# Two buffers for the gate and value rows of a gated MLP's up projection, and their two-column copies on ScalarE

## The chip, the cores and the metric

The kernel runs on one core of a Trainium2 chip. The metric is the device time of one execution in microseconds (us). In the views below PE is TensorE's matmul queue, PEld its weight loads, DVE VectorE, ACT ScalarE, POOL GpSimd and SP the engine that issues the DMAs. L256 is line 256 of the kernel.

## The reference, cut to what matters

One decoder layer: attention and RWKV heads, an output projection, and then a gated MLP with a causal convolution of width 3 over the sequence. The change lies in the MLP alone:

```python
def conv_gated_ffn(h, w_up, conv_w, conv_b, w_down):
    S = h.shape[1]
    u = h @ w_up
    u_pad = jnp.pad(u, ((0, 0), (CONV_WIDTH - 1, 0), (0, 0)))
    u = conv_b + sum(conv_w[j] * u_pad[:, j:j + S] for j in range(CONV_WIDTH))
    gate, val = jnp.split(u, 2, axis=-1)
    return (jax.nn.gelu(gate, approximate=True) * val) @ w_down
```

Sequence 2048, model width 1024, hidden width 4096 for the gate and 4096 for the value, all float32. A float32 product is made of three matmuls on a high and a low part of each operand.

## The kernel before, in words

Phases a and b (projections, attention, RWKV, output projection) fill the first 1200 us. Phase d is the MLP: the up projection until about 2527 us, then the down projection. A framework builds the program: it orders the instructions of each engine by its own scheduler, gives tiles their buffers from pools, and sets the semaphores. Each engine then runs its list in order.

The up projection goes in two halves of the sequence (1024 columns each), and in each half over 32 blocks of 128 hidden features. So there are 64 blocks n. A block has a gate row tile `ug` and a value row tile `uv`, each 128 x 1026: two columns of the half before (the halo of the convolution), then 1024 columns of this half. The 2 x 2 block products are replaced by seven products per block (j = 0 to 6, a Strassen-like scheme), made in the order SEQU = 0, 1, 2, 3, 5, 4, 6. A product (L250) is 12 matmuls of 128x512 into one PSUM bank, so a block is 84 matmuls. Two blocks are interleaved, the second half a block behind the first.

- `wprep(n, j)` prepares the weights of a product: GpSimd makes sums and differences of the loaded weights `wr` (L218, L219, L224, L227), `split` makes a high part on ScalarE (L40, `wh`) and a low part on VectorE (L41, `wl`). It is called 5 products ahead (LEAD). The parts of j = 0, 1, 4, 5 lie in the pool `dwl`, the others in `dwr`.
- `post(n, j)` empties the bank. j = 0, 2, 3: ScalarE copies it to `sum` (L280). j = 1 and 4: VectorE adds `sum` and the bank into the halves of `ug` (L276). j = 5: the same into the second half of `uv`. j = 6 adds to the bank that j = 5 left, and ScalarE copies it to the first half of `uv` (L290). So the product j = 6 of a block can't start before the L276 that reads j = 5 from the same bank.
- `utile(n, b)` takes a buffer for `ug` (b = 0) or `uv` (b = 1) and copies the two halo columns into it (L256). `conv(n, b)` saves the last two columns of the row for the next half (L264, first half of the sequence alone, n < 32), then forms the convolution: ScalarE one tap (L266), VectorE two taps (L267, L268). The gate goes through GELU on ScalarE (L286), and VectorE multiplies gate and value (L293). For each pair of blocks GpSimd and VectorE also form sums for the down projection (L305 to L308).

`ug` and `uv` have one buffer each, in the pool `du`. So `utile` of a block waits for `conv` of the block before to have read the row.

In the first four blocks GpSimd also forms sums of the second half's input (`hsum`, L77 to L83: a load `hs`, four operations, a store). Around the change of the halves (n = 31) the input parts `hh` and `hl` are made anew, by larger splits.

Of the kernel before, what the change touches and what calls it, by code (L numbers as in the profile page):

```python
# [101 lines left out]
def phase_d(ctx, tc, x1, h2t, w_up, cw, halo, w_down, g_post, mhalf, out, hq, act, td):  # L102
# [5 lines left out]
    nc = tc.nc  # L108
    SB = 1024
    NU = FF // P  # L110
    with ExitStack() as es:


        pool = lambda name, bufs=1, side="left": es.enter_context(tc.tile_pool(name=name, bufs=bufs, side=side))
        hrp, wrp, wsp = pool("dr", 2), pool("drw", 2), pool("dsw", 3)
        wps = {"left": pool("dwl", 5)}
        bps = {i: pool(f"d{i}", side="left" if i < 8 else "right") for i in range(14)}
        wps["right"] = pool("dwr", 4, "right")
        up_, ep = pool("du", side="right"), pool("de", side="right")
        pss = [es.enter_context(tc.tile_pool(name=f"dp{i}", bufs=1, space=PSUM)) for i in range(8)]  # L120
        w0c, w1c, w2c, bc = (cw[:, i * 64:(i + 1) * 64] for i in range(4))

# [53 lines left out]
        with ExitStack() as us:  # L176
# [76 lines left out]
            def utile(n, b):  # L253
                col = b * NU + n % NU
                u = up_.tile([P, SB + 2], F32, name="ug" if b == 0 else "uv")
                nc.vector.tensor_copy(out=u[:, 0:2], in_=halo[:, col, :])  # L256
                us_[n, b] = u
                return u

            def conv(n, b):  # L260
                col = b * NU + n % NU
                u = us_.pop((n, b))
                if n < NU:
                    nc.vector.tensor_copy(out=halo[:, col, :], in_=u[:, SB:])  # L264
                y = tp.tile([P, SB], F32, name="yg" if b == 0 else "yv", bufs=3 - 2 * b)
                nc.scalar.activation(out=y, in_=u[:, 2:], func=AF.Identity, scale=w2c[:, col:col + 1], bias=bc[:, col:col + 1])  # L266
                nc.vector.scalar_tensor_tensor(out=y, in0=u[:, 1:SB + 1], scalar=w1c[:, col:col + 1], in1=y, op0=ALU.mult, op1=ALU.add)  # L267
                nc.vector.scalar_tensor_tensor(out=y, in0=u[:, 0:SB], scalar=w0c[:, col:col + 1], in1=y, op0=ALU.mult, op1=ALU.add)  # L268
                return y

            def post(n, j):
# [9 lines left out]
                elif j == 1:  # L281
                    add(utile(n, 0)[:, 2:514], sums.pop((n, 0)), b)
                elif j == 4:
                    add(us_[n, 0][:, 514:], sums.pop((n, 2)), b)
                    ys[n] = conv(n, 0)
                    nc.scalar.activation(out=ys[n], in_=ys[n], func=AF.Gelu_apprx_tanh)  # L286
                elif j == 5:
                    add(utile(n, 1)[:, 514:], sums.pop((n, 3)), a)
                else:
                    nc.scalar.copy(out=us_[n, 1][:, 2:514], in_=a)  # L290
                    yv = conv(n, 1)
                    y = ys.pop(n)
                    nc.vector.tensor_tensor(out=y, in0=y, in1=yv, op=ALU.mult)  # L293
                    k, m = ff // 4, ff // 2 % 2
                    dst = act[half][k][:, m].rearrange("j p t -> p j t")
                    if ff % 2 == 0:
                        nc.sync.dma_start(out=dst[:, 4], in_=y[:, :512])
                        even[0] = y
                        return
                    nc.sync.dma_start(out=dst[:, 5:7], in_=y.rearrange("p (j t) -> p j t", j=2))  # L300

                    e = even.pop(0)
                    s = hrp.tile([P, 4, 512], F32, tag="hr", name="sa")
                    V, Q = nc.vector.tensor_tensor, nc.gpsimd.tensor_tensor
                    Q(out=s[:, 2], in0=e[:, :512], in1=e[:, 512:], op=ALU.subtract)  # L305
                    V(out=s[:, 0], in0=e[:, 512:], in1=y[:, 512:], op=ALU.add)  # L306
                    V(out=s[:, 1], in0=s[:, 0], in1=e[:, :512], op=ALU.subtract)  # L307
                    Q(out=s[:, 3], in0=y[:, :512], in1=s[:, 1], op=ALU.subtract)  # L308
                    nc.sync.dma_start(out=dst[:, 0:4], in_=s)
# [855 lines left out]
def hybrid_layer(ctx, tc, a, c, out):  # L1165
# [25 lines left out]
    phase_b(ctx, tc, s, x, a["w_out"][0], a["norm_mix_post"], a["norm_ffn_pre"], a["sinks"], c["tri"], ident, mhalf, gc, line, x1, h2t, hq[0],  # L1191
            cw, a["conv_w"][0], a["conv_b"][0])
    phase_d(ctx, tc, x1, h2t, a["w_ffn_up"][0], cw, halo, a["w_ffn_down"][0], a["norm_ffn_post"],
            mhalf, out[0], hq, act, td)

# [38 lines left out]
```

## Time and profile before

| | |
|---|---|
| median of 3 runs | 3162.61 us (3157.29 to 3166.73) |
| the profiled execution | 3158.45 us |
| its span on the core | 3156.6 us |
| mean granted clock of TensorE | 0.978 of full speed |
| busy: PE, DVE, ACT, POOL | 3043.6, 2302.4, 1448.5, 1098.2 us |
| share of the span | 96%, 73%, 46%, 35% |

A matmul record is longer than the distance between two matmuls, since they overlap: a busy PE is not a PE at its peak. So the text below counts distances between starts. In a timeline each row has the start, the duration, engine, line and operation, and in brackets the idle time of that engine just before it, with what ended it.

### The profile page before, as it was taken

The page shows a single profiled execution, that of the slowest core. Times are in us where ns is not written, and L with a number is a line of the kernel's source. Part 1 is how long each engine was busy: PE and PEld are TensorE (multiplying, and loading weights), DVE is VectorE, ACT ScalarE, POOL GpSimd, SP SyncE. Part 2 cuts the span into 40 slices and gives each one's busy share as a digit, 9 for nine tenths or more (in the row PEclk, how much of TensorE's full clock was granted, in tenths as well). Part 3 has the DMA queues.
Part 4 walks back from the last instruction along what each step waited for, and adds up shares of the span by engine and source line. Part 5 has one row for each costly group of instructions (what it writes and reads, how often), then busy time and mean ns, then how long its engine had stood idle before and what let it go on. Part 6 is the DMA issues. An engine that isn't in the chain of part 4 may idle for free.

```text
span 3156.6 us, 46475 instructions
## 1 busy us (share of the span) xinstructions
PE 3043.6 (96%) x17897; PEld 2458.3 (78%) x17897; DVE 2302.4 (73%) x3170; ACT 1448.5 (46%) x2438; POOL 1098.2 (35%) x903
## 2 busy tenths in 40 slices
PE   8999999979999998899999999999999999999997
PEld 6788888767777776778787877888887788888786
DVE  6778787766767666999998998888888843334555
ACT  6465756344444445444444445444444432333332
POOL 2212112123323523554444443444444420003642
PEclk9999999969999999999999999999999999999999
DMA  5736363653445635433333343333333474446764
GB/s 162 195 123 187 114 170 104 186 169 108 130 123 161 201 92 196 153 118 101 101 101 101 115 150 123 100 100 100 100 103 101 160 267 151 149 140 227 279 214 167
DMA packets 523762, 461.14 MB, mean 146 GB/s; under 512 B 117306, under 2 KB 405396, under 8 KB 522516
## 3 DMA queue, kind: packets, MB, share of 16 engines
q1 hardware_dynamic: 523540, 458.17, 45.4%
q8 instruction: 140, 2.29, 0.3%
q14 instruction: 82, 0.67, 0.1%
HBM read 316.00 MB, written 142.09 MB: 145 GB/s over the span
## 4 chain that ended last, share of the span: by engine, by line
PE 27%; DVE 18%; DMA 7%; issue 5%; ACT 3%; POOL 0%; SPq 0%; DVEq 0%; POOLq 0%; ACTq 0%
PE b L398 18%; PE b L250 9%; DVE wl L41 7%; DMA wr<-in_w_ffn_up 6%; DVE yg L293 3%; DVE yv L268 2%; ACT yg L266 2%; DVE uv L256 1%; ACT wh L40 1%; DVE ug L276 1%; DVE uv L276 1%; DVE sa L307 0%; DVE sa L306 0%; DVE do L41 0%; DVE yg L267 0%
## 5 line engine op out<-in xcount | busy, mean ns | idle before, releaser
L250 PE MATMUL b<-hh,wh 128*128 128x512 f32 x1792 | 708.9, 396 | 48.0 <-DVE uv L276 33.9
L250 PE MATMUL b<-hh,wl 128*128 128x512 f32 x1792 | 704.8, 394 | 0.5 <-DVE wl L41 0.5
L250 PE MATMUL b<-hl,wh 128*128 128x512 f32 x1792 | 704.7, 393 | 0.2 <-DVE hl L41 0.2
L398 PE MATMUL b<-do 128*128 128x512 f32 x2688 | 613.0, 390 | 5.0 <-DVE do L41 5.0
L398 PEld LDWEIGHTS b<-do 128*128 128x128 f32 x2688 | 506.1, 188 | 111.4 <-DVE do L41 5.9
L41 DVE TENSOR_TENSOR wl<-wr,wh 128x512 fp32r<-128x512 f32 (+1 forms) x400 | 435.1, 1093 | 54.6 <-ACT wh L40 53.3
L250 PEld LDWEIGHTS b<-hh,wh 128*128 128x128 f32 x1792 | 340.3, 190 | 136.7 <-DVE uv L276 47.8
L250 PEld LDWEIGHTS b<-hh,wl 128*128 128x128 f32 x1792 | 339.9, 190 | 74.4 <-DVE wl L41 1.2
L250 PEld LDWEIGHTS b<-hl,wh 128*128 128x128 f32 x1792 | 340.1, 190 | 72.1 <-DVE hl L41 0.6
L41 DVE TENSOR_TENSOR do<-ar,do 128x2048 fp32r<-128x2048 f32 x56 | 138.2, 2467 | 311.4 <-ACT do L40 311.4
L40 ACT CAST wh<-wr 128x512 fp32r<-128x512 f32 (+1 forms) x400 | 274.8, 703 | 172.2 <-PE pj L30 103.5
L218 POOL TENSOR_TENSOR s<-wr 128x512 f32<-128x512 f32 x64 | 131.5, 2054 | 518.1 <-DMA wr<-in_w_ffn_up 518.1
L40 ACT CAST do<-ar 128x2048 fp32r<-128x2048 f32 x56 | 107.1, 1912 | 363.3 <-PE b L398 346.9
L30 PE MATMUL pj<-hh,wh 128*128 128x512 f32 x640 | 256.9, 403 | 4.7 <-ACT hh L40 3.1
L30 PE MATMUL pj<-hh,wl 128*128 128x512 f32 x640 | 255.3, 400 | 0.0
L30 PE MATMUL pj<-hl,wh 128*128 128x512 f32 x640 | 255.0, 400 | 0.0
L161 POOL TENSOR_TENSOR br<-br 128x1024 f32<-128x1024 f32 x32 | 94.9, 2964 | 459.2 <-DMA br<-d_td 358.3
L266 ACT ACTIVATE yg<-ug,cw 128x1024 f32<-128x1024 f32 x64 | 79.7, 1245 | 320.7 <-DVE ug L276 319.0
L40 ACT CAST wh<-s 128x512 fp32r<-128x512 f32 x128 | 79.5, 622 | 189.8 <-POOL s L219 186.4
L30 PEld LDWEIGHTS pj<-hh,wh 128*128 128x128 f32 x640 | 123.0, 192 | 33.3 <-ACT hh L40 3.5
L30 PEld LDWEIGHTS pj<-hl,wh 128*128 128x128 f32 x640 | 122.7, 192 | 26.7
L30 PEld LDWEIGHTS pj<-hh,wl 128*128 128x128 f32 x640 | 122.6, 192 | 26.7
(280 smaller groups left out, 5399.5 us busy)
## 6 DMA issues: line engine op xcount, KB each, us to landing
wr<-in_w_ffn_up SPq DMA_DIRECT2D x128, 512.0 KB
ar<-d_act SPq DMA_DIRECT2D x112, 512.0 KB
br<-in_w_ffn_down SPq DMA_DIRECT2D x72, 512.0 KB
wr<-in_w_in SPq DMA_DIRECT2D x64, 512.0 KB
d_act<-sa SPq DMA_DIRECT2D x32, 1024.0 KB
d_act<-yg SPq DMA_DIRECT2D x32, 512.0 KB
xt<-in_x SPq DMA_DIRECT2D x28, 512.0 KB
d_bk<-bk SPq DMA_DIRECT2D x16, 512.0 KB
```

The lines of the kernel that those rows point to most:

```text
L30: nc.tensor.matmul(out=out, lhsT=a, rhs=b, start=first and i == 0 and j == 0, stop=last and i == n - 1 and j == 2)
L40: nc.scalar.copy(out=hi, in_=raw)
L41: nc.vector.tensor_tensor(out=lo, in0=raw, in1=hi, op=ALU.subtract)
L161: nc.gpsimd.tensor_tensor(out=br[:, 0], in0=br[:, 0], in1=br[:, 1], op=ALU.subtract)
L218: tt(out=r[1], in0=t[:, 2], in1=t[:, 3], op=ALU.add)
L250: nc.tensor.matmul(out=o, lhsT=a[:, k, :], rhs=b[:, k, :], start=j in (0, 1, 3) and k == 0 and i == 0, stop=k == 3 and i == 2, skip_group_ ...
L256: nc.vector.tensor_copy(out=u[:, 0:2], in_=halo[:, col, :])
L266: nc.scalar.activation(out=y, in_=u[:, 2:], func=AF.Identity, scale=w2c[:, col:col + 1], bias=bc[:, col:col + 1])
L268: nc.vector.scalar_tensor_tensor(out=y, in0=u[:, 0:SB], scalar=w0c[:, col:col + 1], in1=y, op0=ALU.mult, op1=ALU.add)
L276: nc.vector.tensor_tensor(out=out, in0=x, in1=y, op=ALU.add)
L293: nc.vector.tensor_tensor(out=y, in0=y, in1=yv, op=ALU.mult)
L398: nc.tensor.matmul(out=bks[n], lhsT=x[:, 2 * h + m, a], rhs=b[:, y], start=k == 0 and p not in CHAIN and m == 0 and j == 0, stop=last and ...
```

## The change: a second buffer for two tiles, one fewer for the weights, and four copies moved

`du` gets two buffers for each of its tiles, so `utile` of a block can take the other one. `dwl` gets four in place of five, for `wh` and for `wl`. The copies of L256 and L264 are ScalarE's.

```diff
-        wps = {"left": pool("dwl", 5)}
+        wps = {"left": pool("dwl", 4)}
...
-        up_, ep = pool("du", side="right"), pool("de", side="right")
+        up_, ep = pool("du", 2, "right"), pool("de", side="right")
...
             def utile(n, b):
                 col = b * NU + n % NU
                 u = up_.tile([P, SB + 2], F32, name="ug" if b == 0 else "uv")
-                nc.vector.tensor_copy(out=u[:, 0:2], in_=halo[:, col, :])
+                nc.scalar.copy(out=u[:, 0:2], in_=halo[:, col, :])
                 us_[n, b] = u
                 return u
...
                 u = us_.pop((n, b))
                 if n < NU:
-                    nc.vector.tensor_copy(out=halo[:, col, :], in_=u[:, SB:])
+                    nc.scalar.copy(out=halo[:, col, :], in_=u[:, SB:])
```

VectorE's list in the first half of the sequence, before, from the product of gate and value of one block (L293) to the convolution of the next block's gate (L267). A number tells a tile from others of its name.

```order
L293 TENSOR_TENSOR yg_15816<-yg_15816,yv_15857 128x1024
L256 COPY uv_15928<-halo_6557 128x2
L41 TENSOR_TENSOR wl_16022<-s_15932,wh_16021 128x512
L276 TENSOR_TENSOR uv_15928<-sum_15887,b_15739 128x512
L306 TENSOR_TENSOR sa_15863<-yg_15665,yg_15816 128x512
L41 TENSOR_TENSOR wl_15979<-wr_15893,wh_15978 128x512
L264 COPY halo_6557<-uv_15928 128x2
L307 TENSOR_TENSOR sa_15863<-sa_15863,yg_15665 128x512
L41 TENSOR_TENSOR wl_15997<-wr_15736,wh_15996 128x512
L276 TENSOR_TENSOR ug_15795<-sum_15837,b_15874 128x512
L264 COPY halo_6557<-ug_15795 128x2
L267 SCALAR_TENSOR_TENSOR yg_15973<-ug_15795,cw_6556,yg_15973 128x1024
```

The same place in the changed program:

```order
L293 TENSOR_TENSOR yg_15816<-yg_15816,yv_15857 128x1024
L41 TENSOR_TENSOR wl_16022<-s_15932,wh_16021 128x512
L306 TENSOR_TENSOR sa_15863<-yg_15665,yg_15816 128x512
L276 TENSOR_TENSOR uv_15928<-sum_15887,b_15739 128x512
L41 TENSOR_TENSOR wl_15956<-wr_15736,wh_15955 128x512
L307 TENSOR_TENSOR sa_15863<-sa_15863,yg_15665 128x512
L276 TENSOR_TENSOR ug_15952<-sum_15909,b_15939 128x512
L41 TENSOR_TENSOR wl_15979<-wr_15893,wh_15978 128x512
L276 TENSOR_TENSOR ug_15795<-sum_15837,b_15874 128x512
L41 TENSOR_TENSOR wl_15997<-wr_15736,wh_15996 128x512
L267 SCALAR_TENSOR_TENSOR yg_15973<-ug_15795,cw_6556,yg_15973 128x1024
```

The three copies are gone. `wl_15956`, which stood ahead of L293 (between the taps L267 and L268 of the value there was `wl_15936`, which now stands behind them), comes behind the addition into `uv`. The first addition into the next gate row `ug_15952`, which stood behind L268 of this gate row, comes ahead of the last addition into `ug_15795`. One L41 now stands between that addition and L267. L306 stands ahead of the addition into `uv`. Blocks of the other kind have no L306 and L307.

ScalarE's list around the gate's first tap (L266), before:

```order
L40 CAST wh_15996<-wr_15736 128x512
L266 ACTIVATE yg_15973<-ug_15795,cw_6556 128x1024
L40 CAST wh_16040<-wr_15736 128x512
L280 COPY sum_15994<-b_15896 128x512
L40 CAST wh_16063<-s_15931 128x512
L290 COPY uv_15928<-b_15739 128x512
L286 ACTIVATE yg_15973<-yg_15973 128x1024
L266 ACTIVATE yv_16014<-uv_15928,cw_6556 128x1024
```

And in the changed program:

```order
L264 COPY halo_6557<-uv_15928 128x2
L40 CAST wh_15978<-wr_15893 128x512
L40 CAST wh_15996<-wr_15736 128x512
L264 COPY halo_6557<-ug_15795 128x2
L266 ACTIVATE yg_15973<-ug_15795,cw_6556 128x1024
L40 CAST wh_16040<-wr_15736 128x512
L280 COPY sum_15994<-b_15896 128x512
L40 CAST wh_16063<-s_15931 128x512
L290 COPY uv_15928<-b_15739 128x512
L286 ACTIVATE yg_15973<-yg_15973 128x1024
L256 COPY ug_16103<-halo_6557 128x2
L266 ACTIVATE yv_16014<-uv_15928,cw_6556 128x1024
```

A copy (L264) now stands just ahead of the gate's first tap, and one (L256) between GELU and the value's first tap. The L264 for `uv` waits for the addition into `uv`, and two L40 stand behind it.

At the start of the up projection SP's list changes too. Before, with a store of `hsum` (L83), the weights of the block n = 4 (L205), and the next load of `hsum` (L77):

```order
L83 DMA d_hq1_83<-hs_14144 128x4x512
L205 DMA wr_14339<-in_w_ffn_up 128x8x128 x2
L297 DMA d_act0_0_84<-yg_14097 128x512
L77 DMA hs_14308<-d_h2t1_81 128x2x1024
L300 DMA d_act0_0_84<-yg_14255 128x2x512
```

And in the changed program:

```order
L83 DMA d_hq1_83<-hs_14144 128x4x512
L297 DMA d_act0_0_84<-yg_14097 128x512
L77 DMA hs_14308<-d_h2t1_81 128x2x1024
L205 DMA wr_14339<-in_w_ffn_up 128x8x128 x2
L300 DMA d_act0_0_84<-yg_14255 128x2x512
```

The weights now stand behind the store of the first product (L297) and the next load of `hsum`. Between about n = 5 and n = 31, and from n = 36 on, the order of the matmuls is the same in both programs.

## Rows read from the trace of the kernel before

**Rows 1.** TensorE's waits in 1243:1420, 1420:1860, 1860:1965 and 1965:2500 (total, times, longest)

```profile
PE b L250 <- DVE uv L276: 10.7, 5, 4.0
...
PE b L250 <- DVE uv L276: 8.1, 11, 1.5
...
PE b L250 <- DVE uv L276: 6.6, 3, 3.7
...
PE b L250 <- DVE uv L276: 7.2, 13, 0.8
```

**Rows 2.** PE's timeline: first of 43 matmuls, the 43rd, and the next

```profile
1599.66 0.39 PE L250 MATMUL b<-hh,wl 128*128 128x512 f32 x1
...
1609.21 0.39 PE L250 MATMUL b<-hh,wl 128*128 128x512 f32 x1
1610.25 0.50 PE L250 MATMUL b<-hh,wh 128*128 128x512 f32 x1 [0.65 <-DVE uv L276]
```

**Rows 3.** VectorE's timeline over two blocks

```profile
1600.28 1.29 DVE L267 SCALAR_TENSOR_TENSOR yv<-uv,cw,yv 128x1024 f32<-128x1024 f32 x1 [0.87 <-ACT yv L266]
...
1602.62 1.28 DVE L268 SCALAR_TENSOR_TENSOR yv<-uv,cw,yv 128x1024 f32<-128x1024 f32 x1
1603.81 1.78 DVE L41 TENSOR_TENSOR wl<-wr,wh 128x512 fp32r<-128x512 f32 x1
1605.52 2.31 DVE L293 TENSOR_TENSOR yg<-yg,yv 128x1024 f32<-128x1024 f32 x1
1607.75 1.26 DVE L256 COPY uv<-halo 128x2 f32<-128x2 f32 x1
1608.92 0.68 DVE L41 TENSOR_TENSOR wl<-s,wh 128x512 fp32r<-128x512 f32 x1
1609.52 0.68 DVE L276 TENSOR_TENSOR uv<-sum,b 128x512 f32<-128x512 f32 x1
...
1613.86 1.28 DVE L267 SCALAR_TENSOR_TENSOR yg<-ug,cw,yg 128x1024 f32<-128x1024 f32 x1 [0.73 <-ACT yg L266]
...
1619.20 1.28 DVE L267 SCALAR_TENSOR_TENSOR yv<-uv,cw,yv 128x1024 f32<-128x1024 f32 x1 [0.87 <-ACT yv L266]
...
1634.15 1.28 DVE L267 SCALAR_TENSOR_TENSOR yg<-ug,cw,yg 128x1024 f32<-128x1024 f32 x1 [0.73 <-ACT yg L266]
...
1639.49 1.28 DVE L267 SCALAR_TENSOR_TENSOR yv<-uv,cw,yv 128x1024 f32<-128x1024 f32 x1 [0.87 <-ACT yv L266]
```

**Rows 4.** GpSimd's timeline over the first of these blocks, and the next L218

```profile
1602.88 2.17 POOL L218 TENSOR_TENSOR s<-wr 128x512 f32<-128x512 f32 x1 [8.71 <-DMA wr<-in_w_ffn_up]
1605.13 1.62 POOL L219 TENSOR_TENSOR s<-s,wr 128x512 f32<-128x512 f32 x1
1606.71 2.27 POOL L224 TENSOR_TENSOR wr<-wr 128x512 f32<-128x512 f32 x1
1608.94 1.79 POOL L305 TENSOR_TENSOR sa<-yg 128x512 f32<-128x512 f32 x1
1611.42 1.68 POOL L227 TENSOR_TENSOR wr<-wr,s 128x512 f32<-128x512 f32 x1 [0.69 <-DVE halo L264]
1621.37 2.15 POOL L218 TENSOR_TENSOR s<-wr 128x512 f32<-128x512 f32 x1 [8.27 <-DMA wr<-in_w_ffn_up]
```

**Rows 5.** VectorE's copies in 1420:1860 by form (busy, mean ns, idle before)

```profile
L256 DVE COPY uv<-halo 128x2 f32<-128x2 f32 x22 | 27.6, 1256 | 0.0
...
L264 DVE COPY halo<-ug 128x2 f32<-128x2 f32 x22 | 12.1, 550 | 0.8
...
L256 DVE COPY ug<-halo 128x2 f32<-128x2 f32 x23 | 3.9, 169 | 0.8
```

**Rows 6.** ScalarE's groups by form over the whole span: one-column copies of phase a

```profile
L580 ACT COPY halo<-ps 128x1 f32<-128x1 f32 x56 | 11.0, 197 | 0.1
```

**Rows 7.** SP's timeline at the start of the up projection

```profile
1283.29 1.00 SPq L205 DMA_DIRECT2D wr<-in_w_ffn_up  x2
...
1286.70 0.38 SPq L77 DMA_DIRECT2D hs<-d_h2t  x1
```

## The prediction, made blind

> **What bounds it now.** I first read TensorE's waits, stage by stage. In the up projection nearly all of its idle time ends with one line: the VectorE addition into `uv` (L276), which reads the bank that the product j = 6 goes on with. It comes to 8.1 us in 11 waits and 7.2 us in 13 in the two long even stretches, and to 10.7 and 6.6 us in the start and in the change of the halves [rows 1]. So in the even stretches there is one wait per two blocks.
>
> TensorE's own timeline gives the floor. 43 matmuls start from 1599.66 to 1609.21, so one is 9.55 / 42 = 0.227 us, and the 168 of two blocks need 38.2 us [rows 2]. VectorE's timeline gives what they take: from one first value tap (L267) to the next but one, 1600.28 to 1639.49, is 39.2 us [rows 3]. A pair loses 1.0 us: the wait of 0.65 [rows 2] and the slower start behind it. In 440 + 535 us there are 24.9 pairs, so 25 us lie there, and 17.3 us of waits in the two irregular stretches.
>
> Then I asked why VectorE is late. Its own list says: from L267 of the value on it never idles until the gate's L267, and then only for ScalarE's first tap [rows 3]. Beside GpSimd's list one sees that the two take turns. L41 started at 1603.81 while L218 ran; L218 ended at 1605.05, L41 at 1605.59. L293 ended 1.08 us behind the end of L219 (1606.75), L256 0.03 us behind the end of L224 (1608.98). In the other direction L219 ends 1.16 us behind that L41 and L224 1.15 us behind L293 [rows 3, 4]. L276, which reads PSUM, took its 0.68 us at 1609.52 with L305 under way. So an operation of one that comes while the other works waits for its end, unless it is L276.
>
> The Trainium skill (SBUF — State Buffer, Who interferes with whom) says this as a rule: GpSimd and VectorE share a port pair under an exclusive lock, and a VectorE instruction with two SBUF inputs waits until a GpSimd instruction that came first has ended. The trace agrees, with the 0.03 and 1.15 us above. By that rule removing a waiting instruction removes no wait, which is the first rival below.
>
> **The copies removed.** By the table 27.6 + 12.1 us in 22 blocks are spent in two of the copies [rows 5], which over 64 blocks would seem to be far more than the whole loss. It isn't so. L256 for `uv` means 1256 ns, but one that meets no GpSimd work means 169 [rows 5]: the rest is waiting for L224. Without it the next L41 starts at the end of L293, waits for the same L224 and ends at 1608.98 + 0.54 = 1609.52, against 1609.60 now. L264 for `ug` (550 ns) lies in the gap in which VectorE waits for L266 anyway, and costs nothing. What the removal itself brings is 0.1 us a block.
>
> **The order.** The second buffer lets the scheduler move two things. L268 of the value comes right behind L267, so VectorE starts taking turns earlier. And the addition into the next `ug` and one L41 change places with the work around the gate. I walk both kinds of block by hand, from L267 of the value at 0, with 0.04 us between dependent instructions, overlaps of 0.08, a turn of GpSimd of 1.15, of L41 0.54, of L293 1.08.
>
> Block without L306: L268 ends at 2.60, where L218 (at 2.60 now, 1602.88 - 1600.28) just about comes first. L218 until 3.75, L41 4.29, L219 5.44, L293 6.52, L224 7.67, L41 8.21, the addition into `uv` 8.81 (9.92 now). Then L305 until 9.36, L41 9.90, the addition into the next `ug` 10.50, L41 11.10, the last addition into this `ug` 11.70. L227 can start at 11.24; no VectorE instruction holds it up, and I give it 1.3 us, between the turn of 1.15 and the 1.68 of its row [rows 4], nearer the first since those 1.68 hold a wait. It ends at 12.54, the last L41 at 13.08. ScalarE in the meantime does L264 and L266 from 11.74. A copy there is 0.2 us long by the one-column copies of phase a [rows 6]; I take 0.1 for its place in the list, since ScalarE instructions overlap by about that, and 0 and 0.2 as ends. L266 is back at 13.1. So L267 of the gate at 13.1, against 13.58 now (1613.86 - 1600.28).
>
> Block with L306 and L307: the same until 8.21. L306 8.81, `uv` 9.41, L41 10.0, L307 10.6, L308 until 11.96, L41 12.50, `ug` 13.10, L227 until 13.95, last L41 14.5. L267 of the gate at 14.5, against 14.95 now (1634.15 - 1619.20) [rows 3].
>
> From the gate's L267 to the value's it is 5.34 us now (1613.86 to 1619.20), and 5.44 with L256 in ScalarE's way, twice. The pair is 13.1 + 14.5 + 10.9 = 38.5 us against 39.2; the floor is 38.2. I take 0.7 of the 1.0 us: 24.9 x 0.7 = 17 us saved. The ends: 25 us if TensorE never waits, nothing if L227 keeps its 1.68 (then both gate taps are 0.38 later and the pair is 39.3).
>
> **ScalarE and the weights.** It was busy 0.46 of the span, and its L264 for `uv` waits for an addition that now ends at 8.81; the two L40 behind it end by 10.0, ahead of the L41 that needs the first at 10.42. That cover is 0.5 us or more; without it the loop grows by what is missing. Four buffers in `dwl` cost nothing: in the order of products four of `dwl` come in each seven, and the fourth back has been used two products (5.4 us) before a new one is due five ahead. Nothing in the trace shows the other case; its end would be an L40 one product late (2.7 us), hidden by those five.
>
> **The irregular stretches.** There VectorE also splits the inputs and GpSimd does `hsum`. The waits for `uv` are 10.7 + 6.6 = 17.3 us [rows 1]. The value rows needn't wait for the taps of the block before, which should take some; the splits stay. Against it stands SP's list: the weights of n = 4, issued at 1283.29, ahead of the `hsum` load at 1286.70, come behind it [rows 7], so some 3.4 us later, and this happens for each of the next loads. I take a third of the 17.3, 6 us saved, with ends of 17 saved and 10 lost (three loads late by 3.4).
>
> **Sum.** The profiled execution took 3158.45 us, 4.2 below the median of the three and inside their range. 3158.45 - 17 - 6 = 3135; since the median lies higher, I say 3136.
>
> **Rivals.**
> - *The wait is handed on.* The L41 behind L293, then the last L41 behind L227, take the waits that the copies had. For it: the step from 1609.60 to 1609.52. Against it: L268 ends 1.0 us earlier in one kind of block (3.62 now, 1603.90 - 1600.28, against 2.60) and the turns shift with it. It decides from L227 at 1.68. Pair 39.2 to 39.3, time 3158, or 3150 with a little from the irregular stretches. Chance 0.20.
> - *TensorE never waits.* L41 behind L268 starts at 2.52, L218 now at 2.60. If L41 is first, L218 goes under it and the block is shorter by 0.6 us: the pair falls under 38.2. Then all 25 us go, and with 17 of the irregular ones 3116. For it: the two are within 0.1 us. Against it: L218 comes from a load released by an L41 whose distance to this place grows with L256 on ScalarE. Chance 0.15.
> - *Slower: GpSimd takes a second turn ahead of the gate's tap.* The last L41 now stands between the addition into `ug` and L267. If L227 isn't done before it, because L305 or L308 is late, VectorE waits for two turns there. Each is 1.15 us in each block. It decides at 0.7 us a pair, where the walk's gain is used up: with a turn in one kind of block the pair is 38.5 + 1.15 = 39.65, in both 40.8, so 24.9 x 0.45 = 11 to 24.9 x 1.6 = 40 us. Time 3169 to 3198. Against it: L227 starts 1.9 us behind the end of L305 and 0.7 behind that of L308. Chance 0.09.
>
> **Chances and range.** The forecast has 0.56, with 3124 to 3148 as its own range. 0.3% (9.5 us) is about what a measurement of this kernel can tell from no change. Faster: the forecast's 0.56, the 0.15 and a little of the first rival, 0.73; same 0.19; slower 0.08. The range 3114 to 3161 takes in the first two rivals and leaves out the third and the tail of the second.
>
> **What would show it.** Right: the addition into `uv` no longer ends TensorE's waits in the even stretches, or for less than 0.3 us per pair; L256 and L264 as ScalarE rows of about 0.2 us; the L41 behind L293 at about 1.2 us and the last one ahead of the gate's L267 at about 1.5, both behind GpSimd; the pair at 38.2 to 38.6. Wrong: the pair still at 39.2 with L41 in the copies' place; or `ug` taps (L266) that start behind L264 by more than 0.2 us; or waits for weights (`wl`, `wh`) at the start, where SP's list changed.

## The result, and the profile after

| | before | after |
|---|---|---|
| median | 3164.67 us (3157.29 to 3166.74, 4 runs) | 3127.78 us (3122.93 to 3128.03, 4 runs) |
| ratio | | 0.9884, 95% interval 0.9864 to 0.9904 |
| span of the profiled execution | 3156.6 us | 3126.1 us |
| mean granted clock | 0.978 | 0.979 |

36.9 us faster; 3136 was forecast, with its own range from 3124 to 3148. The profiled execution of before lies 6.2 us below its median and that of after at its median, so the traces hold 30.5 us of the difference, and the rest isn't in them. Where the time came from is first asked of TensorE's waits by stretch: those of 1243:1420, then of 1860:1965 and of 1965:2500 (total, times, longest). In 1420:1860 there is no row at all.

```profile
PE b L250 <- DVE uv L276: 6.4, 4, 2.8
...
PE b L250 <- ACT sum L280: 1.1, 2, 0.7
...
PE b L250 <- DVE uv L276: 3.3, 1, 3.3
...
PE b L250 <- ACT sum L280: 0.2, 1, 0.2
```

The addition into `uv` ended 32.6 us of waits in 32 places [rows 1]; now it is 9.7 us in 5, none of them in an even stretch (waits too short to be listed aside, see below). VectorE's timeline over two blocks of the kernel after shows how:

```profile
1609.51 1.28 DVE L267 SCALAR_TENSOR_TENSOR yv<-uv,cw,yv 128x1024 f32<-128x1024 f32 x1 [1.75 <-ACT yv L266]
1610.83 1.28 DVE L268 SCALAR_TENSOR_TENSOR yv<-uv,cw,yv 128x1024 f32<-128x1024 f32 x1
1612.04 1.78 DVE L41 TENSOR_TENSOR wl<-wr,wh 128x512 fp32r<-128x512 f32 x1
1613.74 2.31 DVE L293 TENSOR_TENSOR yg<-yg,yv 128x1024 f32<-128x1024 f32 x1
1615.97 1.78 DVE L41 TENSOR_TENSOR wl<-s,wh 128x512 fp32r<-128x512 f32 x1
...
1618.27 0.68 DVE L276 TENSOR_TENSOR uv<-sum,b 128x512 f32<-128x512 f32 x1
...
1624.07 1.28 DVE L267 SCALAR_TENSOR_TENSOR yg<-ug,cw,yg 128x1024 f32<-128x1024 f32 x1
...
1629.51 1.28 DVE L267 SCALAR_TENSOR_TENSOR yv<-uv,cw,yv 128x1024 f32<-128x1024 f32 x1 [1.76 <-ACT yv L266]
...
1642.65 1.28 DVE L267 SCALAR_TENSOR_TENSOR yg<-ug,cw,yg 128x1024 f32<-128x1024 f32 x1
...
1648.10 1.28 DVE L267 SCALAR_TENSOR_TENSOR yv<-uv,cw,yv 128x1024 f32<-128x1024 f32 x1 [1.76 <-ACT yv L266]
```

The hand walk holds to 0.1 us: the gate's L267 comes 14.56 us behind the value's in the block with L306 (14.5 forecast) and 13.14 in the other (13.1), and from there to the next value tap it is 5.44 and 5.45 (5.44). The pair is 38.6 us here, 38.46 to 38.62 over the stretches (38.5). The L41 behind L293 takes 1.78 us, where the copy took 1.26 and that L41 0.68 [rows 3]: the wait for GpSimd's L224 was handed on, as the prediction said. (Its sign for this row, "about 1.2 us", was too small; its own walk has L293 end at 6.52 and that L41 at 8.21.) TensorE still loses something at the same place, too short to be listed as a wait:

```profile
1599.20 0.39 PE L250 MATMUL b<-hl,wh 128*128 128x512 f32 x1
1599.43 0.39 PE L250 MATMUL b<-hh,wl 128*128 128x512 f32 x1
1599.83 0.50 PE L250 MATMUL b<-hh,wh 128*128 128x512 f32 x1
1600.16 0.39 PE L250 MATMUL b<-hl,wh 128*128 128x512 f32 x1
```

The step of 0.40 and the 0.33 behind it, against 0.23, are 0.27 us once in a pair: most of the 0.3 to 0.4 that is left above the floor of 38.2. The copies are ScalarE's, 0.17 to 0.20 us each, and nobody waits for them (by form; ns min/median/max):

```profile
L256 ACT COPY ug<-halo x64: 171/174/195, 1225.5 to 2464.7; 128x2 f32<-128x2 f32 x64
L256 ACT COPY uv<-halo x64: 185/188/193, 1225.6 to 2471.4; 128x2 f32<-128x2 f32 x64
...
L264 ACT COPY halo<-uv x32: 185/192/194, 1267.9 to 1870.9; 128x2 f32<-128x2 f32 x32
```

### The profile page after: what moved, and what is told of

It is laid out like the page before. It is cut to its first block, busy times and chain, and to the rows that moved or that the text cites. A ratio compares the mean times of both kernels' runs of the same rounds, so it can differ in the third digit from the quotient of the medians.

```text
span 3126.1 us, 46445 instructions
## 1 busy us (share of the span) xinstructions
PE 3038.3 (97%) x17897; PEld 2456.2 (79%) x17897; DVE 2296.4 (73%) x2978; ACT 1468.8 (47%) x2630; POOL 1046.5 (33%) x903
## 5 line engine op out<-in xcount | busy, mean ns | idle before, releaser
L41 DVE TENSOR_TENSOR wl<-wr,wh 128x512 fp32r<-128x512 f32 (+1 forms) x400 | 465.4, 1165 | 38.4 <-ACT wh L40 37.7
L41 DVE TENSOR_TENSOR do<-ar,do 128x2048 fp32r<-128x2048 f32 x56 | 134.6, 2404 | 309.9 <-ACT do L40 309.9
L40 ACT CAST wh<-wr 128x512 fp32r<-128x512 f32 (+1 forms) x400 | 272.8, 703 | 135.4 <-PE pj L30 104.3
L40 ACT CAST do<-ar 128x2048 fp32r<-128x2048 f32 x56 | 107.0, 1911 | 362.9 <-PE b L398 352.4
L218 POOL TENSOR_TENSOR s<-wr 128x512 f32<-128x512 f32 x64 | 107.7, 1683 | 463.5 <-DMA wr<-in_w_ffn_up 463.5
L40 ACT CAST wh<-s 128x512 fp32r<-128x512 f32 x128 | 79.5, 622 | 225.6 <-POOL s L219 222.6
L267 DVE SCALAR_TENSOR_TENSOR yv<-uv,cw,yv 128x1024 f32<-128x1024 f32 x64 | 82.8, 1293 | 99.9 <-ACT yv L266 99.9
L41 DVE TENSOR_TENSOR wl<-s,wh 128x512 fp32r<-128x512 f32 x128 | 146.1, 1142 | 12.6 <-ACT wh L40 11.2
L266 ACT ACTIVATE yg<-ug,cw 128x1024 f32<-128x1024 f32 x64 | 79.6, 1244 | 144.3 <-DVE ug L276 144.3
```

The costliest lines, as they stand in the source:

```text
L40: nc.scalar.copy(out=hi, in_=raw)
L41: nc.vector.tensor_tensor(out=lo, in0=raw, in1=hi, op=ALU.subtract)
L218: tt(out=r[1], in0=t[:, 2], in1=t[:, 3], op=ALU.add)
```

## The experiments

The change has four parts: a second buffer for `ug`, one for `uv`, four buffers in place of five for the weights, and the copies on ScalarE. The theories, as the expectations name them: A, the second buffer sets the new order (the prediction's step); B, the four weight buffers set it; C, taking the copies from VectorE is the gain. All runs in one table, with the places of the first value tap (L267 of `yv`) taken from each VectorE timeline: the time of a pair in the two even stretches (blocks 8 to 28 and 34 to 60), and the lengths of the start (blocks 0 to 8) and of the change of the halves (28 to 34). All in us; "d" is the number of buffers in `dwl`. The kernels were timed in groups, each with before beside it; before's median was 3163.5 to 3165.0 us by group, and each ratio is against its own. Of two kernels whose intervals overlap, the order is not shown by the medians alone.

| kernel | median | ratio, interval | start | pair | change | pair |
|---|---|---|---|---|---|---|
| before | 3164 | | 161.9 | 39.26 | 132.5 | 39.07 |
| after | 3127.8 | 0.9884 (0.9864 to 0.9904) | 155.4 | 38.62 | 124.8 | 38.46 |
| both buffers, d 4 | 3128.1 | 0.9886 (0.9872 to 0.9899) | 154.9 | 38.59 | 124.9 | 38.38 |
| copies alone | 3151.3 | 0.9959 (0.9946 to 0.9971) | 158.4 | 39.08 | 130.7 | 39.07 |
| d 4 alone | 3124.4 | 0.9873 (0.9859 to 0.9886) | 161.0 | 37.93 | 127.4 | 37.93 |
| copies, d 4 | 3120.6 | 0.9858 (0.9843 to 0.9873) | 160.2 | 37.95 | 127.7 | 37.99 |
| copies, d 4, `uv` 2 | 3112.5 | 0.9838 (0.9825 to 0.9852) | 153.6 | 37.93 | 124.6 | 38.10 |
| copies, d 5, `uv` 2 | 3147.3 | 0.9948 (0.9935 to 0.9960) | 160.0 | 39.14 | 126.1 | 39.01 |
| d 4, `uv` 2 | 3116.1 | 0.9847 (0.9833 to 0.9860) | 155.9 | 37.93 | 124.9 | 37.98 |
| copies, d 4, `ug` 2 | 3132.7 | 0.9893 (0.9878 to 0.9908) | 156.8 | 38.65 | 127.0 | 38.46 |
| no L224 | 3113.9 | 0.9845 (0.9830 to 0.9861) | 149.9 | 38.14 | 127.0 | 37.97 |
| d 5, both edges | 3148.5 | 0.9946 (0.9933 to 0.9958) | 159.2 | 38.93 | 128.7 | 38.93 |
| d 5, first edge | 3139.8 | 0.9917 (0.9903 to 0.9931) | 157.9 | 38.42 | 130.3 | 38.83 |
| d 5, second edge | 3161.3 | 0.9990 (0.9981 to 0.9998) | 161.4 | 39.67 | 129.7 | 39.35 |

I read a pair below 38.2 as VectorE, late at the end of the start, catching up with TensorE, whose matmuls are no faster there (with d 4 alone 1936 in 440 us, 0.227 each). So stretches of VectorE trade a few us with their neighbours, and the medians decide.

### Both second buffers and four weight buffers, without the copies

```diff
-        wps = {"left": pool("dwl", 5)}
+        wps = {"left": pool("dwl", 4)}
...
-        up_, ep = pool("du", side="right"), pool("de", side="right")
+        up_, ep = pool("du", 2, "right"), pool("de", side="right")
```

> Two buffers for ug and uv and four for the weights of dwl, with the copies left on VectorE. Theory A (the prediction's): the second buffer sets the new order, the copies' own cost is small; theory B: the four weight buffers set the order of the L41, and the second buffer adds little; theory C: taking the copies off VectorE is the gain. A and B: nearly the whole gain, 3126 to 3140 us, a pair of blocks in the even stretches 38.4 to 38.7 us. C: 3150 to 3165 us, pair 39.0 or more.

The time is that of the whole change. So C is not the change's gain.

### The copies alone

```diff
-                nc.vector.tensor_copy(out=u[:, 0:2], in_=halo[:, col, :])
+                nc.scalar.copy(out=u[:, 0:2], in_=halo[:, col, :])
...
-                    nc.vector.tensor_copy(out=halo[:, col, :], in_=u[:, SB:])
+                    nc.scalar.copy(out=halo[:, col, :], in_=u[:, SB:])
```

> The four copies on ScalarE, buffers as before (one for ug and uv, five in dwl). Theories A and B: the L41 behind L293 takes over the wait that L256 had; pair 39.1 to 39.4 us, time 3150 to 3165 us. Theory C (the copies' 47 us of VectorE time in 22 blocks are real work): pair at the floor of 38.3, 3125 to 3140 us.

The pair moves by 0 to 0.2 us. TensorE's waits in 1420:1860 and 1965:2500:

```profile
PE b L250 <- DVE uv L276: 6.5, 11, 0.8
...
PE b L250 <- DVE uv L276: 7.2, 14, 0.8
```

They stand nearly as before [rows 1]: taking away 27.6 + 12.1 us of copies in 22 blocks [rows 5] took away 1.6 us of waits in the first stretch and none in the second. The first rival, the wait handed on, describes this kernel. Of its 12 us the table finds 1.8 in the even stretches and 5.3 in the start and the change of the halves; the rest isn't in the two traces, whose spans differ by 6.8.

### Four weight buffers alone

```diff
-        wps = {"left": pool("dwl", 5)}
+        wps = {"left": pool("dwl", 4)}
```

> Only the pool dwl at four buffers; copies on VectorE, one buffer for ug and uv. Here L268 of the value stands right behind L267 and one L41 behind the addition into uv, as in the changed kernel. Theory A: without the second buffer the waits stay, pair 39.2 us, 3152 to 3165 us. Theory B: by the same walk as in the prediction the pair falls to the floor, 38.0 to 38.4 us, and the time to 3126 to 3142 us. Theory C: no change, 3155 to 3165 us.

The whole gain, from the edit that the prediction had cost at nothing. VectorE's timeline of this kernel from a value tap to the next gate tap:

```profile
1589.32 1.28 DVE L267 SCALAR_TENSOR_TENSOR yv<-uv,cw,yv 128x1024 f32<-128x1024 f32 x1 [0.87 <-ACT yv L266]
1590.64 1.28 DVE L268 SCALAR_TENSOR_TENSOR yv<-uv,cw,yv 128x1024 f32<-128x1024 f32 x1
...
1597.55 0.68 DVE L276 TENSOR_TENSOR uv<-sum,b 128x512 f32<-128x512 f32 x1
1598.15 1.18 DVE L41 TENSOR_TENSOR wl<-wr,wh 128x512 fp32r<-128x512 f32 x1
...
1599.32 0.68 DVE L41 TENSOR_TENSOR wl<-wr,wh 128x512 fp32r<-128x512 f32 x1
1599.92 0.68 DVE L276 TENSOR_TENSOR ug<-sum,b 128x512 f32<-128x512 f32 x1
1600.52 1.47 DVE L41 TENSOR_TENSOR wl<-wr,wh 128x512 fp32r<-128x512 f32 x1
...
1601.98 1.27 DVE L267 SCALAR_TENSOR_TENSOR yg<-ug,cw,yg 128x1024 f32<-128x1024 f32 x1
```

L268 follows L267 at once, and an L41 stands between the last addition into `ug` and the gate's L267. There VectorE idled 0.73 us for ScalarE's tap before [rows 3]; now it works. The gate's L267 comes 12.66 us behind the value's, before 13.58. So the pieces of the new order that the prediction gave to the second buffer are here with one buffer.

### Copies and four weight buffers

The diffs of the two kernels above together.

> The copies on ScalarE and four buffers in dwl, one buffer for ug and uv. Theory A: pair 39.0 us or more, 3148 to 3162 us. Theory B: pair 38.0 to 38.4 us (gate taps at 12.6 and 14.5 us behind the value's, 5.44 us between), 3122 to 3138 us, the same as the changed kernel or a few us faster. Theory C: the same as with the copies alone.

3.8 us below four weights alone; the intervals overlap. The median is also 7 us below that of the whole change, which has the second buffers besides; here too the intervals overlap.

### A second buffer for the value rows alone

The change, with

```diff
-        up_, ep = pool("du", 2, "right"), pool("de", side="right")
+        up_, ep = pool("du", side="right"), pool("de", side="right")
...
-                u = up_.tile([P, SB + 2], F32, name="ug" if b == 0 else "uv")
+                u = up_.tile([P, SB + 2], F32, name="ug" if b == 0 else "uv", bufs=1 + b)
```

> The changed kernel with two buffers for the value rows alone; the gate rows have one again, so that the addition into the next gate row stands in ScalarE's shadow, between L268 and L267, as it does in the kernel with copies and four weight buffers. Theory B (four weight buffers set the place of the L41; the second gate buffer costs 0.5 to 0.65 us a pair; the second value buffer is what helps the start and the change of the halves): pair 37.95 us, the start as long as in the changed kernel (first value tap of block 8 near 1437), time 3108 to 3116. Rival 1, the second gate buffer is what helps in the irregular stretches: the pair is 37.95, the start as with one buffer (1441), time 3118 to 3123. Rival 2, any second buffer costs in the even stretches: pair 38.5, time 3125 to 3130.

The fastest kernel of the study, 52 us below before and 15 below the change. Its windows (length, then PE, PEld, DVE, ACT, POOL busy, granted clock, DMA share, GB/s):

```profile
1420.00:1860.00 440.00, 440.00 (x1936) 363.15 (x1935) 404.20 (x372) 233.71 (x419) 193.68 (x114) 1.00 0.35 115
...
1965.00:2500.00 535.00, 535.00 (x2354) 441.50 (x2353) 481.16 (x437) 270.54 (x432) 237.26 (x134) 1.00 0.36 119
```

TensorE is busy throughout in both, and has no listed wait there. 440 / 1936 is 0.227 us a matmul, 38.2 for 168: the prediction's floor. The addition into the next `ug` stands between L268 and the value's L267 again:

```profile
1615.63 1.27 DVE L268 SCALAR_TENSOR_TENSOR yg<-ug,cw,yg 128x1024 f32<-128x1024 f32 x1
1616.94 0.69 DVE L276 TENSOR_TENSOR ug<-sum,b 128x512 f32<-128x512 f32 x1
1617.54 0.68 DVE L41 TENSOR_TENSOR wl<-s,wh 128x512 fp32r<-128x512 f32 x1
1619.31 1.28 DVE L267 SCALAR_TENSOR_TENSOR yv<-uv,cw,yv 128x1024 f32<-128x1024 f32 x1 [1.08 <-ACT yv L266]
```

VectorE idles 1.08 us there for ScalarE's tap, and in the kernel after 1.75: the second `ug` buffer had taken work out of that shadow and put it ahead of the gate's taps. That is 0.5 us a pair, 12 us in the 23 pairs of the table. Against copies and four weight buffers, which lack only the second value buffer, it is 8 us by the medians; the intervals just overlap.

### The same with five weight buffers

The kernel above with `pool("dwl", 5)`.

> Two buffers for the value rows, the copies on ScalarE, and five weight buffers as before. Theory A, the step of the prediction (a second buffer lets L268 and the L41 change places): pair 38.5 us or less, time 3125 to 3132. Theory B (the cut to four weight buffers does it): L268 stays behind an L41, pair 39.0 to 39.2 us, waits for the uv addition in the even stretches as before; only the irregular stretches gain, some 6 us on the kernel with the copies alone (3151), so 3142 to 3150.

B holds: the pair is as before, with an L41 between the two value taps.

```profile
1597.01 1.28 DVE L267 SCALAR_TENSOR_TENSOR yv<-uv,cw,yv 128x1024 f32<-128x1024 f32 x1 [1.09 <-ACT yv L266]
1598.59 0.69 DVE L41 TENSOR_TENSOR wl<-wr,wh 128x512 fp32r<-128x512 f32 x1 [0.30 <-ACT wh L40]
1599.20 1.28 DVE L268 SCALAR_TENSOR_TENSOR yv<-uv,cw,yv 128x1024 f32<-128x1024 f32 x1
...
1610.40 1.28 DVE L267 SCALAR_TENSOR_TENSOR yg<-ug,cw,yg 128x1024 f32<-128x1024 f32 x1 [1.41 <-ACT yg L266]
```

The gain of 52 us shrinks to 17. A second value buffer without the cut sets no new order.

### The same with four, copies on VectorE

Two value buffers and four weight buffers, without the copies' two lines.

> Two buffers for the value rows, four weight buffers, and both copies on VectorE as before. Theory B with the wait handed on (the copies cost only what GpSimd makes the next VectorE instruction wait anyway): pair 37.9 us, time within 4 us of the kernel with two value buffers and the copies on ScalarE. Rival (taking the copies from VectorE is worth something of its own in the irregular stretches, as the 12 us of the copies alone say): 6 to 12 us slower than that kernel, 3116 to 3126, still with a pair of 37.9.

3.6 us above the fastest kernel, the intervals overlap: beside the new order the copies' place is worth 4 us or less.

### A second buffer for the gate rows alone

As for the value rows, with `bufs=2 - b` (and `bufs=2` for a later tile, `gpost`, that shares the pool's `ug` buffers).

> The changed kernel with two buffers for the gate rows alone, the value rows having one again; four weight buffers and the copies on ScalarE. Theory (the second gate buffer moves the addition into the next gate row from ScalarE's shadow to a place ahead of the gate's taps and costs 0.5 us a pair; the second value buffer helps the irregular stretches by some 8 us): pair 38.5, time 3126 to 3136, so slower than the kernel without any second buffer (3120.6). Rival (the two second buffers help alike in the irregular stretches): 3118 to 3125.

12 us slower than with no second buffer at all, and the pair is that of the change; these intervals don't overlap. The second gate buffer is a loss.

### Without GpSimd's L224

The kernel before without one difference of the weights per block:

```diff
-                    tt(out=t[:, 2], in0=t[:, 0], in1=t[:, 2], op=ALU.subtract)
```

> The kernel before without GpSimd's subtraction L224, which leaves out one difference of the weights per block, so that the products of j = 6 use an unsubtracted piece. It measures the disputed wait by itself. Theory of turns (the copy L256 of the value is long because it waits for the end of L224): L256 uv falls from 1256 to under 300 ns, the addition into uv comes 1.1 us earlier, TensorE's waits for it in the even stretches go, pair 37.9 to 38.2, time 3128 to 3140. Rival (a VectorE copy of two columns is slow or late for another reason, such as the load of the halo or the wait for the product's bank): L256 uv stays at 1.2 us and the time within 0.3% of before.

The line numbers are one lower here; the copy of L256, by form (ns min/median/max):

```profile
L255 DVE COPY uv<-halo x64: 154/156/163, 1219.1 to 2474.8; 128x2 f32<-128x2 f32 x64
```

156 ns in place of 1256 [rows 5], and no listed wait of TensorE in the even stretches, with VectorE's order around the taps as before. So 1.1 us of the copy was the wait for L224, and one GpSimd operation of a block, on an engine busy 35% of the span, was worth 51 us, more than expected; the start is 12 us shorter too. The Trainium skill (SBUF — State Buffer, Who interferes with whom) states the exclusive lock of the two engines on their shared port pair; the 156 ns agree, as did the order of the turns. The prediction's 0.03 us was read on this copy, which has one input; of its rows L41, with two, ended 0.54 us behind L218 [rows 3, 4].

### The order by hand: both edges, and each alone

The kernel before, with its five weight buffers; L41 of j = 0 may not be issued ahead of the value's L268 (first edge), nor that of j = 5 ahead of the addition into `uv` (second edge). Each edge alone is the same with `j == 0` or `j == 5` added to the condition.

```diff
-                split(nc, hi.rearrange("p k f -> p (k f)"), lo.rearrange("p k f -> p (k f)"), src)
+                with tc.issue_after(behind[j].ins) if j in behind else ExitStack():
+                    split(nc, hi.rearrange("p k f -> p (k f)"), lo.rearrange("p k f -> p (k f)"), src)
...
+                if b == 1:
+                    behind[0] = last
...
-                    add(utile(n, 1)[:, 514:], sums.pop((n, 3)), a)
+                    behind[5] = add(utile(n, 1)[:, 514:], sums.pop((n, 3)), a)
```

> The kernel before, with its five weight buffers, one u buffer and the copies on VectorE. Two edges on VectorE's order alone are added: the subtraction L41 of j = 0 of the next block may not be issued ahead of the last value tap (L268), and that of j = 5 not ahead of the addition into uv (L276). That is the order that four weight buffers brought. Theory B1 (the number of buffers acts through this order alone): as with four buffers alone, pair 37.9 to 38.3 us, no wait for the uv addition in the even stretches, time 3116 to 3130. Theory B2 (four buffers act otherwise, by when the copies L40, the loads or GpSimd's turns come): pair 39.0 to 39.3, time 3155 to 3166.

> As the kernel with both edges, with the first alone: L268 of the value follows L267 at once, and both L41 stand between it and L293. If the tap's earlier start is what counts (the step of the prediction: VectorE takes turns earlier), nearly the whole gain: pair 38.0 to 38.4, time 3118 to 3132. If what counts is that one subtraction fewer stands ahead of the uv addition, no gain: the same instructions stand ahead of that addition as before, pair 39.0 to 39.3, time 3152 to 3166.

> As the kernel with both edges, with the second alone: one L41 fewer stands ahead of the uv addition, and an L41 still stands between the two value taps. If what counts is one subtraction fewer ahead of the uv addition: nearly the whole gain, pair 38.0 to 38.4, time 3118 to 3132. If what counts is the tap's earlier start: no gain, pair 39.0 to 39.3, time 3152 to 3166. Halfway if each takes away one turn of GpSimd: 3138 to 3146.

Both expectations for the two edges missed: 38.93 lies between them, near the upper. VectorE's timeline of that kernel (its L270 is L267 of before, L281 is L276, L269 is L266):

```profile
1598.77 1.28 DVE L270 SCALAR_TENSOR_TENSOR yv<-uv,cw,yv 128x1024 f32<-128x1024 f32 x1 [0.87 <-ACT yv L269]
...
1606.05 1.12 DVE L41 TENSOR_TENSOR wl<-s,wh 128x512 fp32r<-128x512 f32 x1 [0.66 <-ACT wh L40]
1607.10 0.68 DVE L281 TENSOR_TENSOR uv<-sum,b 128x512 f32<-128x512 f32 x1
1607.69 1.77 DVE L41 TENSOR_TENSOR wl<-wr,wh 128x512 fp32r<-128x512 f32 x2
...
1609.46 0.68 DVE L41 TENSOR_TENSOR wl<-wr,wh 128x512 fp32r<-128x512 f32 x1
1610.06 0.68 DVE L281 TENSOR_TENSOR ug<-sum,b 128x512 f32<-128x512 f32 x1
...
1612.05 1.28 DVE L270 SCALAR_TENSOR_TENSOR yg<-ug,cw,yg 128x1024 f32<-128x1024 f32 x1 [0.73 <-ACT yg L269]
```

The addition into `uv` is done 9.01 us behind the tap, with four buffers 8.91: for it the edges do what they should. But three L41 now stand between it and the addition into `ug`, with four buffers two, and none is left to fill the 0.73 us of ScalarE's tap. The gate's tap comes at 13.28, with four buffers at 12.66: the 0.62 is one L41. So of the new order's three moves the two that were forced bring about 0.2 us a pair; the third, the L41 behind the addition into `ug`, is what remains. It was not tried by itself, so its share of 1.0 us is read from these two timelines and not shown by a run. The first edge alone does better than both (38.42 and 38.83, where 38.0 to 38.4 or 39.0 to 39.3 was expected), and the second alone gives nothing and a longer pair (39.67 and 39.35). The traces show what the second edge costs. From the kernel with it alone, ScalarE's and VectorE's rows (L221 is L219 of before):

```profile
1610.17 0.62 ACT L40 CAST wh<-s 128x512 fp32r<-128x512 f32 x1 [3.85 <-POOL s L221]
...
1610.82 1.11 DVE L41 TENSOR_TENSOR wl<-s,wh 128x512 fp32r<-128x512 f32 x1 [0.66 <-ACT wh L40]
```

With one L41 fewer ahead of it, VectorE comes to the L41 of `s` too early: its high part waits for GpSimd's L219, and VectorE idles 0.66 us, about what the moved L41 would have taken. In the even stretches this happens in all 46 blocks with the second edge alone, in 20 of them with both edges, and in none before or with the first edge alone. Why GpSimd's turns fall so stays open. What is shown is that the order alone, with five buffers, moves the time by 25 us, and that part of four buffers' gain was not reproduced.

## Why the prediction was right, and where it was not

**Floor and loss: right.** 38.2 us is what TensorE takes where it never waits; the pair lost about 1.0 us before, 0.3 to 0.4 after.

**Why VectorE is late: one reading was wrong.** The prediction has VectorE never idle from the value's L267 to the gate's. In the block shown it idles ahead of the L41 between the two value taps, for ScalarE's high part:

```profile
1602.01 0.69 DVE L41 TENSOR_TENSOR wl<-wr,wh 128x512 fp32r<-128x512 f32 x1 [0.45 <-ACT wh L40]
```

Such waits come to 0.45 us a pair over the even stretches, nearly all in the blocks without L306, where L268 ends 1.0 us later than in the walk: 0.45 is this wait, the rest the L41 itself. So moving that L41 behind L268 removed a wait for ScalarE too, and not only a place in the turns. The walk holds all the same, since it starts from the new order.

**The copies: right.** The removal itself brings nearly nothing in the even stretches, and the run without L224 shows why.

**The walk: right in its numbers.** All its taps came within 0.1 us. Over the 23 pairs of the table the even stretches gave 6.4 + 7.8 = 14.2 us; 17 was forecast for 24.9 pairs, so 0.62 us a pair against 0.7.

**"The second buffer lets the scheduler move two things": wrong.** This step failed in its cause. The cut of `dwl` moved L268 and the L41, with one `u` buffer as with two. The other half of the step, the addition into the next `ug`, is indeed the second buffer's doing, and costs 0.5 us a pair. The walk followed the finished order of the changed program, whatever had set it, so a wrong cause gave a right number.

**"Four buffers in `dwl` cost nothing": wrong in sign.** Alone they gain 39 us. The prediction asked only whether a later buffer makes somebody wait, and not what the buffer had let the scheduler do early: with five, an L41 stood ahead of the taps and the addition for which TensorE waits (the timelines of four weight buffers alone and of five with two `uv` buffers). That the buffers act through this order is shown in part: the order by hand brought 25 us at most of the 39.

**The irregular stretches: the term was too small.** 6 us forecast; the span lost 30.5, so 16 lie outside the even stretches: 6.5 in the start, 7.7 in the change of the halves, the rest at the end. So 3 us too much in the even stretches and 10 too little here leave the sum 7 us off in the profiled executions. The forecast counted only waits for `uv`, of which 10.7 + 6.6 [rows 1] became 6.4 + 3.3; the waits for `sum` in the start fell too, from 4.5 to 1.1 us. The feared loss by SP's order is not seen: from 1243 to 1420 TensorE has no listed wait for `wh` or `wl`, though the weights in question were issued 7.0 us later than before [rows 7], where 3.4 was expected:

```profile
1290.27 1.00 SPq L205 DMA_DIRECT2D wr<-in_w_ffn_up  x2
```

The second value buffer seems to have a part in the gain: with it and without it (3112.5 and 3120.6) the even pairs are nearly alike, and the start and the change are 6.6 and 3.1 us shorter. All four comparisons of the table that differ in it alone go this way, by 4 to 8 us, each with overlapping intervals. What else made up the 16 us was not taken apart.

**Rivals.** The wait handed on is what the copies alone do. TensorE never waiting, 3116, was not this change but is the fastest kernel, at 3112.5, though for another reason than the rival gave: one addition fewer ahead of the gate's tap. Slower, by a second GpSimd turn ahead of that tap: did not come.

## What to carry to other kernels

The number of buffers in a pool is also an input of the scheduler: with more of them it may set work early that nobody needs yet, ahead of what the bound engine waits for, so a smaller pool can be faster. Read the finished order, then change one number at a time, since a second buffer here lost 12 to 15 us for one tile and gained some 4 to 8 for its neighbour. Where two engines take turns, removing a short waiting instruction moves the wait, and removing an operation of the other engine removes it.

## What was not expected of the hardware

A step of TensorE of 0.40 us in place of 0.23, too short to be listed as a wait, was followed by one of 0.33 us in the kernel after. In the kernel before, a step of 1.04 us (from 1609.21 to 1610.25, with the listed wait of 0.65) was followed by one of 0.34 [rows 2]:

```profile
1610.59 0.39 PE L250 MATMUL b<-hl,wh 128*128 128x512 f32 x1
```

So these two stops, long or short, cost another 0.1 us behind them.
